# Loading Silu's table behind the norm's factor column, and spreading layer 0's factor a quarter of v later

## The chip, the cores and the metric

The kernel runs on one core of a Trainium2 chip. The core has five engines with a queue of instructions each: TensorE (PE in the profile, its weight loads PEld), VectorE (DVE), ScalarE (ACT), GpSimd (POOL) and SyncE (SP, which here only issues DMAs). Each engine works off its own queue in order and waits where an input, made by another engine or a DMA, isn't there yet.

The metric is the device time of one execution in microseconds (us). The kernel before was run three times: 654.84, 662.47 and 654.04 us.

## What is computed

A decoder trunk of two layers on one sequence of 256 tokens, with model width 1024, 16 heads of 64, and an FFN of width 2816, all in float32. Layer 0 mixes tokens by attention with forget gates, layer 1 by block-sparse attention with a relative-position bias. Each layer is, in short:

```python
u = rmsnorm(h, attn_norm_g[i])
h = h + attention_i(u) @ w_o
u = rmsnorm(h, ffn_norm_g[i])
gu = u @ ffn_w_in[i]
h = h + (silu(gu[..., :D_FF]) * gu[..., D_FF:]) @ ffn_w_out[i]
gate = sigmoid(rmsnorm(h, ple_norm_g[i]) @ ple_w_gate[i])
h = h + gate * (p[i] @ ple_w_up[i])
```

and a last rmsnorm makes the output. The norm is `y = x * rsqrt(mean(x*x) + eps) * g`: one factor for each token, and one gain for each feature.

## The kernel before

**Layout and precision.** Activations are kept feature by token: `h` is 128 partitions x 8 tiles x 256 tokens. Each float32 operand is split in a high part, rounded to a shorter format (`whi`, or `hi` of an activation), and a low part, the rest (`wlo`, `lo`); a product is then three matmuls, high x high, high x low and low x high (`mm3`, lines 90 to 92). For each weight tile of 128 x 1024 SP loads it into `raw` (six buffers), ACT rounds it to `whi` (line 152) and DVE subtracts it to `wlo` (line 153); `whi` and `wlo` have six buffers each, so this runs some tiles ahead of TensorE.

**The norm.** `Norm` works around the factor's late arrival. The matmuls run on h times gain alone (`block`, `pair`), without the factor. The factor comes later: `square` sums the squares on ACT and DVE, and `root` (line 207) sums over the partitions with two tiny matmuls into the bank `ss`, brings mean and epsilon together on DVE (`ms`), and raises it to the power -0.5 on POOL, into `col` (line 216): one factor for each token, tokens on the partitions. Where tokens lie along the free dimension, the factor has to be laid out as a row on all partitions: `spread` (line 218) multiplies the column, broadcast, by the identity on TensorE into the bank `pr`, and copies the bank twice into `row`, scaled on ACT (line 226) and plain on DVE (line 227).

**Layer 0's v and forget gates.** `attention` (line 381) first computes v with a loop over c = 0 to 3, two weight tiles each: a quarter of v's reduction per turn, 24 matmuls of 512 columns. In layer 0, at the end of the turn c = 1, `mid` (this is `fox_bias`) multiplies out the forget gates into the bank `pf`, the four squares run, and then `root`, `spread(-0.125)` and `small(done)`; the last issues three small loads on ACT's queue, behind the last square. After the loop `rest()` makes the gates' running sum from `pf` and `row` by a chain of DVE and ACT operations (lines 320 to 334), and v is copied out of its banks times `col` (line 414). In layer 1 `root` stands at the end of c = 2 and `spread` behind the whole loop. The projections of q and k then multiply by `row` (line 437), and the scores add the forget gates' sum (line 338).

**The FFN.** `ffn` (line 566) goes over 22 feature tiles f. The first two are computed together in `up([0, 1])`: four weight tiles, a loop over k, then `nm.root()` (line 583). `up([2])` then runs one weight tile (24 matmuls), `spread` (line 593), and `gated(*early)` for f = 0 and 1. `gated` multiplies the bank by the row into `gut` (DVE, line 600), applies Silu into `sg` (ACT, line 603), multiplies by the other half (DVE, line 604), and splits the product into high and low (`fp`, ACT line 261 and DVE line 262). `down(f)` then multiplies it into the banks `fo`.

**ACT's tables.** ACT evaluates a function by a table; the compiler puts a load of the table (ACT_TABLE_LOAD) ahead of the first operation that needs another one. `table(func, after)` (line 100) is an activation of one column into a scratch column, `warm`, whose only purpose is to have the load at that place; with `after` it reads the column given, and so waits for it. It is used for Exp at the start and behind the running sum, and for Sigmoid in both gates, right behind their `root` (lines 686 and 724). For Silu there is none: the load stands ahead of the first Silu of each layer.

**What sets the order.** A planner orders each engine's queue. It takes instructions in the order of the program where their inputs are ready by its own estimate, and lets a later one go ahead where an earlier one's input isn't. So an engine's queue follows the program only nearly: TensorE's two products of layer 0's spread stand two matmuls of v behind those of `ss`, though they follow directly in the program. `tc.issue_after` binds an instruction behind another on its engine.

Of the kernel before, what the change touches and what calls it, by code (L numbers as in the profile page):

```python
# [29 lines left out]
AF = mybir.ActivationFunctionType  # L30
# [41 lines left out]
def trunk(ctx: ExitStack, tc: tile.TileContext, xh, xg, wx, xr, pt, w, cst, gf, rel, hot, rvm, out):  # L72
# [7 lines left out]
    def bank(name):  # L80
        return ps.tile([P, 512], F32, tag="bank", name=name)
# [6 lines left out]
    def mm3(o, a, b, start, stop):  # L88
        (ah, al), (bh, bl) = a, b
        mm(o, ah, bh, start=start, stop=False, skip_group_check=True)  # L90
        mm(o, ah, bl, start=False, stop=False, skip_group_check=True)  # L91
        mm(o, al, bh, start=False, stop=stop, skip_group_check=True)  # L92
# [7 lines left out]
    def table(func, after=None):  # L100

        nc.scalar.activation(warm, ones if after is None else after, func)
# [20 lines left out]
    def half(at=0, entry=0):  # L123


        i = state["next"]
        state["next"] += 1
        if i not in (1, 2):
            raw = work.tile([P, HW + LINE], F32, tag="raw", bufs=RAW, name=f"raw{i}")
        ht, lt = (work.tile([P, HW + 2 * LINE], F32R, tag=n, bufs=6, name=f"{n}{i}") for n in ("whi", "wlo"))  # L130
        hi, lo = ht[:, at:at + HW], lt[:, at:at + HW]
        if entry:
            nc.sync.dma_start(raw[:, 0:HW], w[i - 2][:, 0:HW])
            nc.scalar.activation(hi, raw[:, 0:HW], AF.Copy)
            ats = [(at + FURTHER, 0, entry), (at + LINE, entry, HW)]
            for a, c0, c1 in ats:
                nc.vector.tensor_tensor(lt[:, a + c0:a + c1], raw[:, c0:c1], f32(hi[:, c0:c1]), op=ALU.subtract)
            return hi, [lt[:, a + k * P:a + (k + 1) * P] for a, c0, c1 in ats for k in range(c0 // P, c1 // P)]
        if i in (1, 2):
            raw = hw[:, i - 1, S:]  # L140
        parts = 2 if i < 2 else 1
        for q in range(parts):
            c = slice(q * HW // parts, (q + 1) * HW // parts)
            if i in (1, 2):
                at = slice(c.start + (S if q else 0), c.stop + S)
                nc.sync.dma_start(hw[:, i - 1, at], wx[i - 1][:, at])
            else:
                nc.sync.dma_start(raw[:, c], w[max(i - 2, 0)][:, c])
            if i + q == 0:
                nc.vector.tensor_copy(hi[:, c], raw[:, c])  # L150
            else:
                nc.scalar.activation(hi[:, c], raw[:, c], AF.Copy)  # L152
            nc.vector.tensor_tensor(lo[:, c], raw[:, c], f32(hi[:, c]), op=ALU.subtract)  # L153
        return hi, lo

    def blocks(entry=()):

        hi, lo = half(APART, len(entry) * P)
        return [[t[k] if isinstance(t, list) else t[:, k * P:(k + 1) * P] for k in range(KT)] for t in (hi, lo)]
# [72 lines left out]
    nm = Norm(0)  # L232
# [27 lines left out]
    def split(hi, lo, src):  # L260
        nc.scalar.activation(hi, src, AF.Copy)  # L261
        nc.vector.tensor_tensor(lo, src, f32(hi), op=ALU.subtract)  # L262

    def tokens(o, x, t, w, start, stop):

        at = slice(t * P, (t + 1) * P)
        mm3(o, (x[0][:, at], x[1][:, at]), w, start, stop)
# [10 lines left out]
    def residual(b, bk):  # L278
        at = h[:, 2 * b:2 * b + 2].rearrange("p k s -> p (k s)")
        nc.vector.tensor_tensor(at, at, bk, op=ALU.add)  # L280

    def feat(bks, m, w, x, start, stop):

        mm3(bks[m // 2][:, m % 2 * S:(m % 2 + 1) * S], w, x, start and m % 2 == 0, stop)
# [3 lines left out]
    def small(after):  # L288
        with tc.issue_after(after.ins):
            for t, a in ((rl, rel), (ht, hot), (rm, rvm)):  # L290
                nc.scalar.dma_start(t, a)
# [81 lines left out]
    def enter(bks, x, w):  # L373

        for hf in range(2):
            for a, b in ((0, 0), (1, 0), (0, 1)):
                for t in range(2):
                    mm(bks[2 * t + hf], x[a][:, t * P:(t + 1) * P], w[b][:, hf * HC:(hf + 1) * HC],
                       start=a == b, stop=False, skip_group_check=True)

    def attention(layer, nm, mid, early, nf):
        vb = [bank(f"v{layer}_{b}") for b in range(4)]
        rest = None
        for c in range(4):
            wt = [early.pop(0) if early else half() for _ in range(2)]
            for kk in range(2):
                hi, lo = wt[kk]
                k = 2 * c + kk
                if early and k == 0:
                    enter(vb, nm.k(0), wt[0])  # L390
                    continue
                for t in range(2):
                    for hf in range(2):
                        cols = slice(hf * HC, (hf + 1) * HC)
                        tokens(vb[2 * t + hf], nm.k(k), t, (hi[:, cols], lo[:, cols]), k == 0, k == KT - 1)
            if layer == 0 and c == 1:
                rest = mid(nm)
                for b in range(4):
                    done = nm.square(b)
                nm.root()  # L400
                nm.spread(-0.125)
                small(done)
            if layer == 1:
                moba[1](c)
            if layer == 1 and c == 2:
                nm.root()
# [159 lines left out]
    def ffn(layer, nm, filler, np_):  # L566
        acc = []
        prod = {}

        def up(fs):  # L570

            bks = {f: bank(f"gu{layer}_{f}") for f in fs}

            def step(f, a, wt, k, start):
                mm3(bks[f][:, a * S:(a + 1) * S], (wt[0][k], wt[1][k]), nm.k(k), start, k == KT - 1)

            if fs[0] == 0:
                wts = {f: (blocks(), blocks()) for f in fs}
                for k in range(KT):
                    for f in fs:  # L580
                        for a in range(2):
                            step(f, a, wts[f][a], k, k == 0 and a == 0)
                nm.root()
                return fs, bks
            for a in range(2):
                if fs[0] == 2 and a:
                    wt = gapped()
                else:
                    wt = blocks()
                for k in range(KT):  # L590
                    step(fs[0], a, wt, k, k == 0)
                if fs[0] == 2 and a == 0:
                    nm.spread()
                    gated(*early)
            gated(fs, bks)

        def gated(fs, bks):
            for f in fs:
                t = work.tile([P, 2, S], F32, tag="t2k", bufs=3, name=f"gut{layer}_{f}")
                nc.vector.tensor_tensor(t.rearrange("p a s -> p (a s)"), bks[f],  # L600
                                        nm.row.rearrange("p a s -> p (a s)"), op=ALU.mult)
                sg = work.tile([P, S], F32, tag="sg", name=f"sg{layer}_{f}")
                nc.scalar.activation(sg, t[:, 0], AF.Silu)
                nc.vector.tensor_tensor(sg, sg, t[:, 1], op=ALU.mult)  # L604
                both = work.tile([P, 2, S], F32R, tag="fp", bufs=4, name=f"fp{layer}_{f}")
                split(both[:, 0], both[:, 1], sg)
                prod[f] = both[:, 0], both[:, 1]

        def down(f):
            hi, lo = blocks()  # L610
            for m in range(KT):
                feat(acc, m, (hi[m], lo[m]), prod[f], f == 0, False)

        early = up([0, 1])
        acc.extend(bank(f"fo{layer}_{b}") for b in range(4))
        for f in range(2, FT, 2):
            up([f])
            up([f + 1])
            if f == FT - 6:
                pp = filler()  # L620
            if f < FT - 2:
                down(f - 2)
                down(f - 1)
        filler(pp)
        for b in range(4):
            hi, lo = blocks()
            for i in range(4):
                for n in range(2):
                    w = hi[2 * i + n], lo[2 * i + n]
                    feat(acc, 2 * b + n, w, prod[FT - 4 + i], False, i == 3)  # L630
            residual(b, acc[b])
            np_.pair(b)
        for b in range(4):
            np_.square(b)
# [163 lines left out]
    for layer in range(2):  # L798
# [8 lines left out]
        if layer == 0:  # L807
            nm = Norm(3)
# [126 lines left out]
```

## Time and profile before

| | us |
|---|---|
| runs | 654.84, 662.47, 654.04 (median 654.84) |
| profiled execution, its own time | 660.64 |
| its span, first to last instruction | 658.6 |
| TensorE busy in the span | 648.4 |
| weight loads (PEld) busy | 627.1 |
| DVE busy | 450.9 |
| ACT busy | 374.4 |
| POOL busy | 13.6 |

The profile is of one execution; times within it are from the start of its span. TensorE was granted 0.997 of its clock. A row of a timeline has the start, the duration, the engine, the line of the kernel, the operation with output and inputs, and the number of like operations that were merged; in brackets the idle time of the engine before it and what ended it. Back-to-back operations overlap a little, so durations in a row can add up to more than the distance of the starts. The rows of waits have who waited, on which line, for whom, the time in all, how often, and the longest.

The places that the change touches are early in layer 0 (from 16 to 45 us) and the start of each FFN (from 124 to 145 us, and from 440 to 461 us).

### The profile page before, as it was taken

What the parts mean: (1) busy time and instruction counts of PE and PEld (TensorE: products, weight loads), DVE (VectorE), ACT (ScalarE), POOL (GpSimd) and SP (SyncE); (2) the same over time, 40 slices, a digit from 0 to 9 for tenths busy, and PEclk for the clock granted to TensorE, in tenths of its full rate; (3) what the DMA queues carried; (4) which work ended last, traced back from release to release, by engine and by line L of the source; (5) the groups of instructions that cost most, each with busy time, mean ns of one, the idle gap of its engine ahead of it and who ended that gap; (6) DMA issues with size and microseconds to landing.
All of it is one profiled execution on the core that took longest, in us unless ns stands there. A gap on an engine that the chain in (4) does not pass through costs nothing.

```text
span 658.6 us, 13220 instructions
## 1 busy us (share of the span) xinstructions
PE 648.4 (98%) x5392; PEld 627.1 (95%) x5392; DVE 450.9 (68%) x723; ACT 374.4 (57%) x634; POOL 13.6 (2%) x21
## 2 busy tenths in 40 slices
PE   9999999999999999999999999999999999999995
PEld 7799999999999999999989999999999999999984
DVE  6788884786666666667796888568666556566765
ACT  6676674664444445455865677557444444444763
POOL 1000000000000000000001000000000000000001
PEclk9999999999999999999999999999999999999998
DMA  9888544386666666656487544447656656666501
GB/s 348 289 276 264 202 128 159 101 262 191 192 195 201 189 196 217 192 166 192 161 292 261 182 135 128 130 128 229 190 188 190 180 182 190 191 209 186 166 1 64
DMA packets 35883, 124.15 MB, mean 189 GB/s; under 512 B 3888, under 2 KB 6256, under 8 KB 35696
## 3 DMA queue, kind: packets, MB, share of 16 engines
q1 hardware_dynamic: 35408, 122.92, 58.8%
q8 instruction: 42, 0.69, 0.4%
q10 hardware_dynamic: 416, 0.40, 0.2%
q14 instruction: 17, 0.14, 0.1%
HBM read 122.24 MB, written 4.22 MB: 192 GB/s over the span
## 4 chain that ended last, share of the span: by engine, by line
PE 95%; issue 3%; ACT 1%; DVE 1%; POOL 0%; POOLq 0%; ACTq 0%
PE gu L90 12%; PE gu L92 12%; PE gu L91 12%; PE fo L91 6%; PE fo L92 6%; PE fo L90 6%; PE pq L90 5%; PE pq L91 4%; PE pq L92 4%; PE wo L90 2%; PE wo L91 2%; PE wo L92 2%; PE v L90 2%; PE v L92 2%; PE v L91 2%
## 5 line engine op out<-in xcount | busy, mean ns | idle before, releaser
L153 DVE TENSOR_TENSOR wlo<-raw,whi 128x1024 fp32r<-128x1024 f32 (+1 forms) x207 | 251.2, 1219 | 131.8 <-ACT whi L152 131.4
L152 ACT ACTIVATE whi<-raw 128x1024 fp32r<-128x1024 f32 (+1 forms) x206 | 216.0, 1055 | 181.4 <-PE gu L91 79.1
L90 PE MATMUL gu<-g,whi 128*128 128x256 f32 x704 | 196.2, 279 | 0.0
L92 PE MATMUL gu<-g,wlo 128*128 128x256 f32 x704 | 195.8, 278 | 0.0
L91 PE MATMUL gu<-g,whi 128*128 128x256 f32 x704 | 195.8, 278 | 0.0
L91 PEld LDWEIGHTS gu<-g,whi 128*128 128x128 f32 x704 | 133.5, 190 | 0.0
L90 PEld LDWEIGHTS gu<-g,whi 128*128 128x128 f32 x704 | 132.2, 188 | 0.0
L92 PEld LDWEIGHTS gu<-g,wlo 128*128 128x128 f32 x704 | 132.2, 188 | 0.0
L91 PE MATMUL fo<-fp,whi 128*128 128x256 f32 x352 | 98.3, 279 | 0.1
L92 PE MATMUL fo<-fp,wlo 128*128 128x256 f32 x352 | 98.0, 279 | 0.0
L90 PE MATMUL fo<-fp,whi 128*128 128x256 f32 x352 | 98.0, 278 | 0.0
L90 PE MATMUL pq<-g,whi 128*128 128x256 f32 x256 | 71.7, 280 | 0.0
L91 PE MATMUL pq<-g,whi 128*128 128x256 f32 x256 | 71.0, 277 | 0.0
L92 PE MATMUL pq<-g,wlo 128*128 128x256 f32 x256 | 71.0, 277 | 0.0
L91 PEld LDWEIGHTS fo<-fp,whi 128*128 128x128 f32 x352 | 66.8, 190 | 0.6 <-DVE fp L262 0.5
L90 PEld LDWEIGHTS fo<-fp,whi 128*128 128x128 f32 x352 | 66.1, 188 | 0.0
L92 PEld LDWEIGHTS fo<-fp,wlo 128*128 128x128 f32 x352 | 66.1, 188 | 0.0
L90 PEld LDWEIGHTS pq<-g,whi 128*128 128x128 f32 x256 | 48.2, 188 | 1.1 <-issue 0.6
L91 PEld LDWEIGHTS pq<-g,whi 128*128 128x128 f32 x256 | 48.2, 188 | 0.0
L92 PEld LDWEIGHTS pq<-g,wlo 128*128 128x128 f32 x256 | 48.1, 188 | 0.0
L261 ACT ACTIVATE fp<-sg 128x256 fp32r<-128x256 f32 x44 | 18.1, 415 | 45.9 <-DVE sg L604 45.9
L600 DVE TENSOR_TENSOR gut<-gu,row 128x512 f32<-128x512 f32 x44 | 30.0, 690 | 14.8 <-PE gu L92 14.8
(176 smaller groups left out, 970.2 us busy)
## 6 DMA issues: line engine op xcount, KB each, us to landing
raw<-w SPq DMA_DIRECT2D x206, 512.0 KB, 4.3
raw<-w SPq DMA_DIRECT2D x7, 540.0 KB, 5.2
d<-d SPq DMA_DIRECT2D x4, 768.0 KB, 9.7
bias<-d SPq DMA_DIRECT2D x4, 512.0 KB, 6.7
h<-xh SPq DMA_DIRECT2D x1, 1024.0 KB, 9.9
hw<-wx SPq DMA_DIRECT2D x1, 640.0 KB, 5.8
hw<-xr SPq DMA_DIRECT2D x1, 640.0 KB, 7.7
raw<-w SPq DMA_DIRECT2D x2, 256.0 KB, 3.2
```

The source lines that it names most:

```text
L90: mm(o, ah, bh, start=start, stop=False, skip_group_check=True)
L91: mm(o, ah, bl, start=False, stop=False, skip_group_check=True)
L92: mm(o, al, bh, start=False, stop=stop, skip_group_check=True)
L152: nc.scalar.activation(hi[:, c], raw[:, c], AF.Copy)
L153: nc.vector.tensor_tensor(lo[:, c], raw[:, c], f32(hi[:, c]), op=ALU.subtract)
L261: nc.scalar.activation(hi, src, AF.Copy)
L600: nc.vector.tensor_tensor(t.rearrange("p a s -> p (a s)"), bks[f], nm.row.rearrange("p a s -> p (a s)"), op=ALU.mult)
```

## The change

Two edits:

- In layer 0, `spread(-0.125)` moves from the end of the turn c = 1 to the end of the turn c = 2: in the program its two products, and the two copies into `row`, now stand behind the 24 matmuls of that quarter of v. `root` and `small(done)` stay at the end of c = 1.
- In `up([0, 1])`, behind `root`, `table(AF.Silu, nm.col[:, 0:1])` is added: an activation of one column that reads the norm's factor column. It is there once in each layer's FFN.

```diff
@@ attention
                 for b in range(4):
                     done = nm.square(b)
                 nm.root()
+                small(done)
+            if layer == 0 and c == 2:
                 nm.spread(-0.125)
-                small(done)
             if layer == 1:
                 moba[1](c)
             if layer == 1 and c == 2:
@@ ffn, up
                         for a in range(2):
                             step(f, a, wts[f][a], k, k == 0 and a == 0)
                 nm.root()
+                table(AF.Silu, nm.col[:, 0:1])
                 return fs, bks
             for a in range(2):
                 if fs[0] == 2 and a:
```

## The prediction

> **What bounds the kernel now.** I read the busy shares and the chain that ended last, then who TensorE waited for, and then the timelines of the places the change touches, engine by engine. From the page:
>
> ```profile
> span 658.6 us, 13220 instructions
> PE 648.4 (98%) x5392; PEld 627.1 (95%) x5392; DVE 450.9 (68%) x723; ACT 374.4 (57%) x634; POOL 13.6 (2%) x21
> PE 95%; issue 3%; ACT 1%; DVE 1%; POOL 0%; POOLq 0%; ACTq 0%
> ```
>
> TensorE is the bound: 98% busy, 95% of the chain. The change removes no matmul, so it can only win time in which TensorE stands still: 658.6 - 648.4 = 10.2 us in all. The waits of TensorE's weight loads name the two places that the change touches:
>
> ```profile
> PEld pr L223 <- POOL col L216: 1.8, 1, 1.8
> PEld fo L91 <- DVE fp L262: 0.5, 2, 0.3
> ```
>
> One wait for the factor column in layer 0, and two short ones, one in each FFN, for the first product's low half. Everything the change can directly win is in these two rows.
>
> **Part A, the spread of layer 0, a quarter of v later.** TensorE's timeline around it (start, duration, idle before in brackets), then POOL, ACT and DVE at the same place:
>
> ```profile
> 20.98 0.39 PE L91 MATMUL v<-wlo,g 128*128 128x512 f32 x1
> 21.21 0.50 PE L212 MATMUL ss<-first_line,sq 128*128 128x1 f32 x4
> 21.57 0.49 PE L92 MATMUL v<-whi,g 128*128 128x512 f32 x1
> 21.90 0.40 PE L91 MATMUL v<-wlo,g 128*128 128x512 f32 x1
> 23.67 0.71 PE L223 MATMUL pr<-con,col 128*128 128x128 f32 x4 [1.38 <-POOL col L216]
> 24.14 0.48 PE L92 MATMUL v<-whi,g 128*128 128x512 f32 x1
> ```
>
> ```profile
> 22.06 1.56 POOL L216 TENSOR_TENSOR col<-ms,nhalf 128x2 f32<-128x2 f32 x1 [9.72 <-DVE ms L214]
> ```
>
> ```profile
> 18.68 1.04 ACT L152 ACTIVATE whi<-raw 128x1024 fp32r<-128x1024 f32 x1
> 24.42 0.38 ACT L226 ACTIVATE row<-pr 128x256 f32<-128x256 f32 x1 [4.69 <-PE pr L223]
> ```
>
> ```profile
> 21.83 2.36 DVE L153 TENSOR_TENSOR wlo<-raw,whi 128x1024 fp32r<-128x1024 f32 x2
> ```
>
> The products pr stand two v matmuls behind ss on TensorE, but POOL needs until 22.06 + 1.56 = 23.62 for the column. A v matmul follows the last one after 21.21 - 20.98 = 0.23 us; so without pr the next would start at 21.90 + 0.23 = 22.13 instead of waiting to 23.67: a stall of 1.54 us (the row's 1.38 counts from the modelled end). The four pr records themselves take 24.14 - 23.67 = 0.47 us; that is moved, not removed.
>
> After the change 24 v matmuls of two weight tiles (k = 4 and 5) rank ahead of pr, and 15 of them (3 of k = 4, 12 of k = 5) are still to run at 21.57, which is 15 x 0.23 = 3.4 us: pr comes at about 25.1, 1.5 us after the column. Is the work that fills the hole ready? The weights' high parts are (ACT finished k = 5 and 6 by 19.72 and then stood for 4.69 us); the low part of k = 5 is the first of the two subtractions at 21.83, ready at about 21.83 + 2.36/2 = 23.0, and TensorE asks for it after the rest of k = 4 and the four matmuls by whi of k = 5, at 22.13 + 0.23 + 4 x 0.23 = 23.3. So the fill holds with 0.3 us to spare. Layer 1 already has its spread a quarter of v behind its root, and there pr waits for nothing:
>
> ```profile
> 349.44 0.61 PE L223 MATMUL pr<-con,col 128*128 128x128 f32 x4
> ```
>
> What is late then: the row (ACT copy, DVE copy) about 1.5 us later, hence the forget-gate chain behind it, which ends in the cast of c on POOL and is first read by the scores:
>
> ```profile
> 36.48 0.29 POOL L334 CAST c<-c 128x128 fp32r<-128x128 f32 x1 [12.87 <-DVE c L333]
> ```
>
> ```profile
> 44.34 0.33 PE L338 MATMUL sp<-c,sel 64*128 64x384 f32 x2
> ```
>
> There are 44.34 - 36.77 = 7.6 us of cover; a gain of 1.5 and a row 1.5 us later leave some 4.6. On ACT's queue the conversion of k = 7 is no longer bound to stand behind the row's copy; if it still does, it starts 1.5 us later, at about 26.2, its subtraction ends near 28.5, and TensorE asks for that low half at about 25.6 + 12 x 0.23 + 0.23 = 28.6. Tight, but covered. The three small loads of `small` keep their place behind the last square, ahead of the row's copy, on ACT's queue; SP's and POOL's lists are not touched. A: -1.54. Its bounds are 0 (pr is put back where it was) and -1.8 (all that the weight-load row shows); I take -1.54, since it comes from the spacing of the matmuls themselves.
>
> **Part B, Silu's table.** ACT, POOL, DVE and TensorE in the FFN of layer 0:
>
> ```profile
> 127.89 3.91 ACT L152 ACTIVATE whi<-raw 128x1024 fp32r<-128x1024 f32 x4 [5.00 <-PE gu L91]
> 132.18 1.06 ACT L152 ACTIVATE whi<-raw 128x1024 fp32r<-128x1024 f32 x1 [0.38 <-PE gu L91]
> 133.14 0.36 ACT L226 ACTIVATE row<-pr 128x256 f32<-128x256 f32 x1
> 135.39 1.07 ACT L152 ACTIVATE whi<-raw 128x1024 fp32r<-128x1024 f32 x1 [1.88 <-PE gu L91]
> 136.47 1.28 ACT L603 ACT_TABLE_LOAD   x1
> 137.77 0.73 ACT L603 ACTIVATE sg<-gut 128x256 f32<-128x256 f32 x2
> 138.40 1.05 ACT L152 ACTIVATE whi<-raw 128x1024 fp32r<-128x1024 f32 x1
> ```
>
> ```profile
> 130.36 1.61 POOL L216 TENSOR_TENSOR col<-ms,nhalf 128x2 f32<-128x2 f32 x1 [93.59 <-DVE ms L214]
> ```
>
> ```profile
> 128.98 1.23 DVE L153 TENSOR_TENSOR wlo<-raw,whi 128x1024 fp32r<-128x1024 f32 x1 [3.97 <-ACT whi L152]
> ```
>
> ```profile
> 135.07 1.88 DVE L600 TENSOR_TENSOR gut<-gu,row 128x512 f32<-128x512 f32 x3
> 136.86 1.21 DVE L153 TENSOR_TENSOR wlo<-raw,whi 128x1024 fp32r<-128x1024 f32 x1
> 138.22 0.76 DVE L604 TENSOR_TENSOR sg<-sg,gut 128x256 f32<-128x256 f32 x2
> 139.48 1.23 DVE L153 TENSOR_TENSOR wlo<-raw,whi 128x1024 fp32r<-128x1024 f32 x1 [0.49 <-ACT whi L152]
> 140.62 0.75 DVE L262 TENSOR_TENSOR fp<-sg,fp 128x256 fp32r<-128x256 f32 x2
> ```
>
> ```profile
> 140.74 0.28 PE L90 MATMUL fo<-fp,whi 128*128 128x256 f32 x1
> 141.09 0.39 PE L91 MATMUL fo<-fp,whi 128*128 128x256 f32 x1
> ```
>
> The load (1.28 us) stands ahead of the first Silu, and TensorE then waits: half of the 0.5 us in the waits row above, 0.25 us per layer, is all that a perfect move can win. But DVE, not ACT alone, carries this stretch: from 128.98 to 140.62 it rests only where the load has held ACT. With 1.14 us between a subtraction and the next start (140.62 - 139.48) those rests are 138.22 - 138.00 = 0.22 and, taking the pair at 138.22 as 0.67 less overlap, 139.48 - 138.89 = 0.59: 0.81 us to reclaim.
>
> What does the load cost at its new place? The gates of layer 0 have the same form already (four weight tiles, root, table on the column, one more tile, spread), with Sigmoid:
>
> ```profile
> 314.26 2.96 ACT L152 ACTIVATE whi<-raw 128x1024 fp32r<-128x1024 f32 x3 [6.94 <-PE pg L91]
> 317.23 1.28 ACT L102 ACT_TABLE_LOAD   x1
> 318.53 0.20 ACT L102 ACTIVATE first_line<-col 128x1 f32<-128x1 f32 x1
> ```
>
> ```profile
> 315.35 1.23 DVE L153 TENSOR_TENSOR wlo<-raw,whi 128x1024 fp32r<-128x1024 f32 x1 [5.91 <-ACT whi L152]
> ...
> 322.32 1.88 DVE L674 TENSOR_TENSOR pgt<-pg,row 128x512 f32<-128x512 f32 x3
> ```
>
> There the load falls behind the third of four conversions, and DVE's first product by the row starts 322.32 - 315.35 = 6.97 us behind its first subtraction; in the FFN it is 135.07 - 128.98 = 6.09. So the load at its new place delays DVE by 0.88 us. Behind it on ACT's queue stand the fourth conversion (a tile for o, not needed before 140.74), the next one and the row's copy; behind those on DVE the four subtractions' last, the row's second copy and gut; SP's next loads into raw come as much later, with several tiles in hand. The wait on col is covered: the load ends at about 130.83 + 1.28 = 132.11 and the column is there at 130.36 + 1.61 = 131.97. Later the 0.81 us come back, so fp's low half moves by 0.88 - 0.81 = +0.07 us per layer, +0.15 for both. The added activation (0.20 us, twice) lies in ACT's idle time of 1.88 us. Bounds: -0.5 (both stalls gone) and +1.8 (twice 0.88, nothing reclaimed); I take +0.15, from the nearest row, the Sigmoid load.
>
> The Trainium skill (ScalarE: Activation LUTs, What ACT_TABLE_LOAD costs) adds a drain of about 1380 ns to the 1283 ns of each load. The trace has the 1.28 us but no drain: the next activation starts 0.02 us behind the load, in the FFN and in the gates. By the page's total of 2.66 us the early load would hold ACT 1.38 us longer in each layer, an estimate of +2.8 us over both, and the sum would be +1.4 instead of -1.4.
>
> **The sum.** -1.54 + 0.15 = -1.4 us. The profiled execution took 660.64 us, its span 658.6; they would become 659.2 and 657.2. It is slower than the median of the runs, 654.84 (654.04 to 662.47), by a difference that lies in no stage of the change; against the median I predict 654.84 - 1.4 = 653.4.
>
> **The rivals.**
> 1. Both parts pay in full: the load slips into idle time and DVE loses nothing. -1.54 - 0.48 = -2.0: 652.8. Against it: the 0.88 us of the gates.
> 2. The move does nothing: the planner orders by when it believes inputs ready (pr stands two matmuls behind ss, though POOL takes 1.56 us) and puts pr into a gap that it sees early, right behind the four whi matmuls of k = 5 or sooner. A falls toward 0, B stays: 655.0. For it: TensorE's order there is the planner's, not the program's. Against it: in layer 1 a lower rank was enough.
> 3. Slower: the load goes behind the second conversion instead of the third. ACT then waits for the column to 131.97, the third conversion ends at about 133.1 instead of 130.8, and gut starts near 136.9, 1.83 us later instead of 0.88; with 0.81 reclaimed each layer loses 1.0, so -1.54 + 2.0 = +0.5: 655.3; one conversion earlier still, 657.5. It decides from gut 1.6 us late, where 2 x (1.6 - 0.81) exceeds A. Against it: the same distance of 1.1 us from the first conversion to ss in gates and FFN.
> 4. The load holds ACT for longer than its row shows, as by a drain. If that doubled it, 2 x 1.28 us would be added: 656.0. Against it: the 0.02 us behind each load.
>
> **How the numbers follow.** My forecast has 5 in 10, the first rival 1.5, the second 1.5, the third 1.2, the fourth 0.2; 0.6 is left for another order further on. All of them lie within 4 us, less than what separates two runs of one kernel here. So the range is set by these: from the fastest run with the full gain, 654.04 - 2.0 = 652.0, to the profiled execution with the third rival's loss, 660.64 + 0.5 = 661.1. Two per cent, about what a measurement of this kernel can tell from no change, is 13.1 us; no case reaches it, so faster has 0.01, slower 0.02, and within it 0.97.
>
> **What would show it.** Right: the row "pr from col" is gone from TensorE's waits, v matmuls follow ss without a gap, and the ACT idle of 4.69 us ahead of the row's copy is gone; in each FFN the load stands behind three conversions on L102, gut starts about 0.9 us later against the first subtraction, and the wait of fo for fp is still there at 0.25 to 0.4 us. Wrong: pr still waiting for the column, a new wait of v for wlo at k = 5 or 7, gut more than 1.6 us late, or fo waiting for nothing.

## The result, and the profile after

Twenty executions of the changed kernel took 653.59 us in the median (652.74 to 654.11). Twenty of the kernel before, taken beside them, took 655.46 (654.04 to 663.6). The ratio is 0.9939 (95% interval 0.9913 to 0.9965): faster by about 0.6%, clear of no change, and under the 2% that was named beforehand. I had forecast 653.4 us and a difference of 0.2%. Ratios, here and below, are of means, and leave out executions more than 1.5% above the fastest of their kernel.

The medians hide the form of the difference. The executions of the kernel before lie on two levels: 13 of the 20 between 654.04 and 656.75, seven between 660.31 and 663.6. All 20 of the changed kernel lie within 1.4 us. The means are 657.55 and 653.56, 4.0 us apart. The profiled execution of before (660.64 us) was one of the upper level; that of the changed kernel took 654.03.

The page of the changed kernel, its span and the busy time of each engine:

```profile
span 652.0 us, 13223 instructions
PE 642.4 (99%) x5392; PEld 620.9 (95%) x5392; DVE 450.4 (69%) x723; ACT 375.3 (58%) x636; POOL 13.6 (2%) x21
```

The span fell by 6.6 us (658.6 to 652.0), and TensorE's busy time by 6.0 (648.4 to 642.4), with the same 5392 matmuls. So the time in which TensorE stood still fell by only 0.6 us, from 10.2 to 9.6; the rest is that its matmuls took less time. No sum over waits can show that.

**Where it went.** TensorE's timeline where layer 1's FFN starts and ends its products, before:

```profile
456.73 0.28 PE L90 MATMUL fo<-fp,whi 128*128 128x256 f32 x1
457.08 0.38 PE L91 MATMUL fo<-fp,whi 128*128 128x256 f32 x1
457.31 0.28 PE L92 MATMUL fo<-fp,wlo 128*128 128x256 f32 x1
...
609.71 0.40 PE L90 MATMUL pu<-whi,phi 128*128 128x512 f32 x1
```

And after:

```profile
456.43 0.28 PE L90 MATMUL fo<-fp,whi 128*128 128x256 f32 x1
456.55 0.28 PE L91 MATMUL fo<-fp,whi 128*128 128x256 f32 x1
456.66 0.28 PE L92 MATMUL fo<-fp,wlo 128*128 128x256 f32 x1
...
603.31 0.40 PE L90 MATMUL pu<-whi,phi 128*128 128x512 f32 x1
```

Before, the second product `fo` waits for `fp`, and the three products take 457.31 - 456.73 = 0.58 us against 0.23 after: the wait costs 0.35 us. But from the first `fo` to the first `pu` it is 152.98 us before and 146.88 after: 6.10 less, of which the wait explains 0.35. The other 5.75 us are spread evenly over the FFN. TensorE's windows (stretch, its length, busy time and number of matmuls, granted clock, DMA share, GB/s) show it. The first row is in layer 0's FFN, the two others in layer 1's; before:

```profile
160.00:180.00 20.00, 20.00 (x179) 1.00 0.61 188
485.00:505.00 20.00, 20.00 (x172) 1.00 0.62 186
560.00:580.00 20.00, 20.00 (x172) 1.00 0.67 203
```

After:

```profile
160.00:180.00 20.00, 20.00 (x179) 1.00 0.61 189
485.00:505.00 20.00, 20.00 (x179) 1.00 0.66 199
560.00:580.00 20.00, 20.00 (x179) 1.00 0.68 202
```

At the same granted clock of 1.00, and with TensorE busy throughout, the same matmuls run 172 to a window in the one and 179 in the other. (A window also counts the two or three that reach into it.) From start to start that is 0.118 us against 0.113, 4%. Some 1300 matmuls (152.98 / 0.118) times 4.5 ns are the 5.8 us. In this window layer 0 ran at 0.113 in both profiles. So TensorE has two steady rhythms here, and layer 1 of the profiled execution of before fell into the slower one where `fo` had waited.

The slower rhythm is no rarity. It also stands, for a short while, at the start of every FFN, between the small products `ss` of `root` and the products `pr` of `spread`. TensorE before, in layer 0, behind `ss` (which starts at 128.83 us):

```profile
129.39 0.28 PE L91 MATMUL gu<-g,whi 128*128 128x256 f32 x1
...
131.98 0.28 PE L92 MATMUL gu<-g,wlo 128*128 128x256 f32 x1
132.10 0.64 PE L223 MATMUL pr<-con,col 128*128 128x128 f32 x4
...
132.69 0.28 PE L91 MATMUL gu<-g,whi 128*128 128x256 f32 x1
...
140.29 0.28 PE L92 MATMUL gu<-g,wlo 128*128 128x256 f32 x1
```

From 129.39 to 131.98 us there are 22 distances of 0.118 us, and from 132.69 to 140.29 there are 67 of 0.113. The 13 profiles of this document have 26 FFNs. In all 26 the row of matmuls goes over to the slower rhythm at `ss`, and in 23 it is back on the faster one behind `pr`.

**Part A.** The changed kernel's TensorE around the spread:

```profile
21.54 0.50 PE L212 MATMUL ss<-first_line,sq 128*128 128x1 f32 x4
...
22.46 0.40 PE L92 MATMUL v<-whi,g 128*128 128x512 f32 x1
23.99 0.49 PE L223 MATMUL pr<-con,col 128*128 128x128 f32 x2 [1.14 <-POOL col L216]
24.24 1.17 PE L90 MATMUL v<-whi,g 128*128 128x512 f32 x4
25.24 0.38 PE L223 MATMUL pr<-con,col 128*128 128x128 f32 x2
...
43.77 0.49 PE L451 MATMUL sp<-qkt 64*128 64x128 f32 x4
```

The spread's two products have come apart. The first stands one v matmul later than before and still waits for `col`; the second stands behind the four products by `whi` of k = 5. From `ss` to the first scores it is 43.77 - 21.54 = 22.23 us. Before, the scores' first row was

```profile
43.66 0.49 PE L450 MATMUL sp<-qkt 64*128 64x128 f32 x4
```

which is 43.66 - 21.21 = 22.45 us behind its `ss`. The move won 0.22 us where I had forecast 1.54.

**Part B.** ACT of the changed kernel in layer 0's FFN:

```profile
127.99 2.96 ACT L152 ACTIVATE whi<-raw 128x1024 fp32r<-128x1024 f32 x3 [5.00 <-PE gu L91]
130.96 1.28 ACT L102 ACT_TABLE_LOAD   x1
132.25 0.20 ACT L102 ACTIVATE first_line<-col 128x1 f32<-128x1 f32 x1
```

DVE at the same place:

```profile
129.08 1.23 DVE L153 TENSOR_TENSOR wlo<-raw,whi 128x1024 fp32r<-128x1024 f32 x1 [3.96 <-ACT whi L152]
...
136.05 1.28 DVE L602 TENSOR_TENSOR gut<-gu,row 128x512 f32<-128x512 f32 x2
137.25 0.42 DVE L606 TENSOR_TENSOR sg<-sg,gut 128x256 f32<-128x256 f32 x1
137.58 0.69 DVE L602 TENSOR_TENSOR gut<-gu,row 128x512 f32<-128x512 f32 x1
138.18 0.42 DVE L262 TENSOR_TENSOR fp<-sg,fp 128x256 fp32r<-128x256 f32 x1
```

And TensorE:

```profile
140.84 0.28 PE L90 MATMUL fo<-fp,whi 128*128 128x256 f32 x1
140.95 0.28 PE L91 MATMUL fo<-fp,whi 128*128 128x256 f32 x1
```

The load stands behind three conversions, and `gut` starts 136.05 - 129.08 = 6.97 us behind the first subtraction: exactly the gates' distance, 0.88 more than before. What follows on DVE is another order, though. Before it was three `gut`, a subtraction, both `sg`, another subtraction and then `fp`, at 140.62. Now the chain of f = 0 goes straight through, two `gut`, `sg`, `gut`, `fp`, and `fp` starts at 138.18, 2.8 us ahead of the product that reads it (140.95). `fo` waits for nothing, in both layers.

### The profile page after: what moved, and what is told of

Same layout as the page of the kernel before. It is cut to its first block, busy times and chain, and to the rows that moved or that the text cites. A ratio compares the mean times of both kernels' runs of the same rounds, so it can differ in the third digit from the quotient of the medians.

```text
span 652.0 us, 13223 instructions
## 1 busy us (share of the span) xinstructions
PE 642.4 (99%) x5392; PEld 620.9 (95%) x5392; DVE 450.4 (69%) x723; ACT 375.3 (58%) x636; POOL 13.6 (2%) x21
## 4 chain that ended last, share of the span: by engine, by line
PE 96%; issue 3%; ACT 0%; POOL 0%; POOLq 0%; DVE 0%; ACTq 0%
PE gu L92 12%; PE gu L90 12%; PE gu L91 12%; PE fo L92 6%; PE fo L90 6%; PE fo L91 6%; PE pq L90 5%; PE pq L92 5%; PE pq L91 4%; PE wo L90 2%; PE wo L91 2%; PE wo L92 2%; PE v L90 2%; PE v L91 2%; PE v L92 2%
```

## The experiments

All ran beside the kernel before. Over all of this, 129 executions of the kernel before are on record; 80 took up to 657.61 us, and 49 from 659.86 up, three of these over 667. "Upper" below means 658.5 us or more. The medians and the counts have all executions.

| run | median (lowest to highest, n) | upper | ratio to before |
|---|---|---|---|
| changed kernel | 653.59 (652.74 to 654.11, 20) | 0 | 0.9939 [0.9913, 0.9965] |
| e1, table alone | 654.29 (653.44 to 655.56, 12) | 0 | 0.9958 [0.9926, 0.9989] |
| e2, spread alone | 655.04 (653.95 to 666.96, 12) | 5 | 1.0012 [0.9975, 1.0048] |
| e3, spread bound | 652.43 (651.82 to 652.94, 12) | 0 | 0.993 [0.99, 0.996] |
| e4, table in layer 1 alone | 654.87 (654.07 to 656.51, 12) | 0 | 0.9964 [0.993, 0.9998] |
| e5, table in layer 0 alone | 654.9 (653.99 to 667.41, 12) | 2 | 0.9957 [0.9921, 0.9994] |
| e6, low half late by 3.1 us | 660.49 (658.2 to 665.93, 12) | see text | 1.0049 [1.0006, 1.0092] |
| e7, column later | 656.8 (655.72 to 658.2, 12) | 0 | 0.9974 [0.9939, 1.0008] |
| e8, low half late by 1.1 us | 661.98 (654.63 to 667.95, 12) | 10 | 1.0024 [0.9975, 1.0074] |
| e9, break in layer 1 | 659.55 (658.37 to 665.59, 12) | see text | 1.0028 [0.9992, 1.0063] |
| e10, changed kernel again | 653.79 (653.37 to 660.81, 12) | 1 | 0.9942 [0.9907, 0.9978] |
| e11, e3 again | 652.37 (651.5 to 652.9, 12) | 0 | 0.9923 [0.9891, 0.9954] |

### Each part alone (e1 and e2)

e1 is the kernel before with the table's line, e2 the kernel before with the spread moved:

```diff
 e1: in up([0, 1])
                 nm.root()
+                table(AF.Silu, nm.col[:, 0:1])
 e2: in attention
+                small(done)
+            if layer == 0 and c == 2:
                 nm.spread(-0.125)
-                small(done)
```

> The Silu table alone; layer 0's spread stays behind c = 1. Theory (the low half of fp no longer makes fo wait, and with that wait TensorE's drop into its slower matmul rhythm, 117.8 instead of 113.3 ns, in layer 1's FFN is gone): no row of fo waiting for fp; 113.3 ns from 455 to 600 us; every execution between 652.5 and 654.5 us, none near 661; median 653.5, like the changed kernel. Rival (the shift of the spread is what keeps the slower rhythm away): two levels as before, near 654.5 and 661, the upper one in about 8 of 20.

> The later spread alone, no Silu table. Theory: fo waits for fp in both layers as before, 0.25 us each; two levels as before, near 654.5 and 661, the upper in a third or so of the executions; pr still waits for the column, 1.0 to 1.6 us. Rival (the spread keeps the slower rhythm away): one level, at 653 to 654.

The table alone took the upper level away: 0 of 12 against 49 of 129. The spread alone did not: 5 of 12, and its lower executions, 654.64 in the median, stand 0.5 us below the 655.1 of the kernel before. For the upper level both theories hold. e1's times came out higher than expected: the median is 0.8 us above the 653.5 expected, and five executions lie above 654.5. In e1's profile another cost of the old place of the spread showed up. TensorE's windows there:

```profile
24.00:26.00 2.00, 2.00 (x8) 0.59 0.82 260
26.00:28.00 2.00, 2.00 (x6) 0.55 0.75 238
28.00:30.00 2.00, 2.00 (x11) 1.00 0.78 199
```

The fourth column is the granted clock. Behind the wait for `col` it falls to 0.59 and 0.55 for the better part of 4 us, and six to eight v matmuls run in 2 us instead of ten to twelve. Neither profile of before and after has this drop; e4's has it. So the old place costs more than its wait in some executions.

### The spread where the diff says (e3 and e11)

The changed kernel, with the spread's instructions bound behind the last matmul of the turn c = 2 (`mm3` and `tokens` are made to return their last matmul):

```diff
-                        tokens(vb[2 * t + hf], nm.k(k), t, ...)
+                        last = tokens(vb[2 * t + hf], nm.k(k), t, ...)
...
             if layer == 0 and c == 2:
-                nm.spread(-0.125)
+                with tc.issue_after(last.ins):
+                    nm.spread(-0.125)
```

> The changed kernel with both pr products bound behind the last v matmul of c = 2 (issue_after on TensorE), so that the planner cannot put one of them into an earlier gap. Theory (the changed kernel's part A gains nothing, since one pr product still waits for the column): no wait of pr for the column; 1.2 to 1.5 us faster than the changed kernel, median 652.2. Rival (the v matmuls behind it then wait for their low halves on DVE instead, or the forget-gate chain is late): no gain, 653.5.

> e3 once more, on the same chip as e10. Theory (part A pays once both products are behind the quarter of v): 1.2 to 1.4 us below e10, as the distance from ss to the first scores (22.23 against 20.82 us) says. Rival (e3's lower time came from another chip): same as e10 within 0.3 us.

TensorE's timeline of e3:

```profile
21.58 0.50 PE L212 MATMUL ss<-first_line,sq 128*128 128x1 f32 x4
...
25.25 0.39 PE L92 MATMUL v<-whi,g 128*128 128x512 f32 x1
25.48 0.61 PE L223 MATMUL pr<-con,col 128*128 128x128 f32 x4
...
42.41 0.49 PE L452 MATMUL sp<-qkt 64*128 64x128 f32 x4
```

Both products stand together behind the quarter of v and wait for nothing. From `ss` to the first scores it is 42.41 - 21.58 = 20.83 us: 1.62 less than before, 1.40 less than in the changed kernel. The medians follow: 652.43 against the 653.59 of the result, which were measured apart, and 652.37 against 653.79, which were measured together on one chip. This is the fastest of the versions measured. The prediction's price for the move was right; the diff alone did not make the move.

### The table in one layer only (e4 and e5)

Both take e1 and load the table early in one of the layers:

```diff
                 nm.root()
-                table(AF.Silu, nm.col[:, 0:1])
+                if layer == 1:        # e4;  layer == 0 in e5
+                    table(AF.Silu, nm.col[:, 0:1])
```

> The Silu table in layer 1's FFN only, spread as before. Theory, if the drop into the slower rhythm happens in layer 1 only: one level, about 0.2 us over the table in both layers, 653.7. If the wait in layer 0 can cause it too, its FFN has some 1400 matmuls behind that wait: an upper level some 6 us higher in a part of the executions.

> The Silu table in layer 0's FFN only, spread as before. Theory (the wait of fo for fp in layer 1 is what can drop TensorE into the slower rhythm of 117.8 ns until the FFN ends): the upper level near 661 is back, in a third or so of the executions; the lower one near 654.7. Rival (the table as such, in either layer, keeps it away): one level near 654.7.

With the wait gone from layer 1 alone, none of 12 is on the upper level. Its median of 654.87 is 1.2 above what I expected; the four executions from 656.18 up have a mean granted clock of 0.993 or 0.994, as e1's two with the clock drop. That layer 0's wait by itself does not bring the upper level rests on these 12 executions, since no other kernel here keeps that wait alone. With the wait gone from layer 0 alone, two are: 661.52 and 667.41. Two of 12 is fewer than the kernel before has (49 of 129), but too few to tell the two shares apart. What speaks more is the profile of the execution at 667.41, which has 173 matmuls at 160 to 180 us and 172 at 485 to 505: both layers on the slower rhythm. In layer 0, where `fo` does not wait, the slower rhythm of the stretch behind `ss` stayed on behind `pr`. So the wait is not the only place that decides.

### A wait put back (e6 and e8)

The changed kernel, with the low half of layer 1's first `fp` held back by a short chain on POOL. Two of its columns are multiplied by one, so the values stay; e6 multiplies five times, e8 once:

```diff
+        def late(lo):
+            one2 = tiny.tile([P, 2], F32, bufs=1, name="one2")
+            nc.gpsimd.tensor_scalar(one2, f32(lo), 0.0, 1.0, op0=ALU.mult, op1=ALU.add)
+            nc.gpsimd.tensor_tensor(one2, one2, nhalf, op=ALU.pow)
+            for _ in range(5):        # once in e8
+                nc.gpsimd.tensor_tensor(lo, f32(lo), one2, op=ALU.mult)
...
+                if layer == 1 and f == 0:
+                    late(both[:, 1, 0:2])
```

> The changed kernel, tables in both layers, but in layer 1 the low half of f = 0 passes through seven small POOL operations that multiply two of its columns by one, some 2.8 us, so that fo has to wait for it again, by 0.2 to 0.7 us; TensorE, ACT and DVE have the same instructions in the same order as in the changed kernel. Theory (the wait itself, not the place of the table, causes the slower rhythm): an upper level some 6 us over the lower appears in a third or so of the executions; the lower one near 654.0. Rival (it hangs on the order of ACT and DVE): one level, near 654.0.

> As e6, with one POOL multiplication of the low half instead of five, so that fo waits some 0.4 us in layer 1 instead of 3.1, and the granted clock has no reason to fall. Order of TensorE, ACT and DVE as in the changed kernel. Theory (a short wait of fo is enough to start the slower rhythm): lower level 653.6 to 654.3, upper level some 5.75 us above it, in 2 to 7 of 12. Rival (it takes the long wait, or the old order of DVE and ACT): one level at 653.6 to 654.3.

e6's chain was longer than meant, since the five multiplications of two columns took 3.30 us on POOL: `fo` waited for 3.1 us, and the clock fell to 0.57 in the window from 460 to 464 us. Its 12 executions form two groups of six, 658.2 to 658.64 and 662.35 to 665.93. The first holds the wait and the clock drop, and the profiled execution, one of this group (658.31), has layer 1 on the faster rhythm, with 179 matmuls at 485 to 505 us: a long wait need not start the slower one. The second group has more, but e6 mixes too much to be read.

e8 has the wait without the clock drop. Its wait, in the waits of TensorE's weight loads:

```profile
PEld fo L91 <- POOL fp L603: 1.1, 1, 1.1
```

Ten of 12 executions lie above 659.9, and two at 654.63 and 655.65; the last are near what the changed kernel and 1.1 us give (654.7). So two executions lie 1 to 2 us above the changed kernel's median, and ten lie 6 to 14 above it, where I had expected 2 to 7 of 12. The windows of the profiled one, at 667.95:

```profile
160.00:180.00 20.00, 20.00 (x173) 1.00 0.58 184
485.00:505.00 20.00, 20.00 (x172) 1.00 0.57 185
```

The granted clock is 1.00 in both, so this is no drop of the clock. This execution had both layers on the slower rhythm, as e5's had: in layer 0 it stayed on behind `pr`, and in layer 1 it was gone behind `pr` and came back at the added wait. Of the other nine only the time is known, so in which layer each of them was slow is not shown. But layer 0 has the changed kernel's code, and that kernel has one upper execution in 32 (e10), so I put most of the ten down to the wait in layer 1.

### The column later still (e7)

e1, with layer 0's factor column computed twice on POOL, the first time into a column that nobody reads, so that the old spread waits longer:

```diff
+            if n == 0:
+                twice = tiny.tile([P, 2], F32, bufs=1, name="twice")
+                nc.gpsimd.tensor_tensor(twice, ms, nhalf, op=ALU.pow)
             nc.gpsimd.tensor_tensor(self.col, ms, nhalf, op=ALU.pow)
```

> The table in both layers, spread as before, and layer 0's first column is computed twice on POOL, one behind the other, so that pr waits 1.56 us longer, about 3.1 us in all. Theory (the wait for the column can make the granted clock fall to about 0.55 for some 3.4 us behind it, which costs 1.6 us and happened in part of the executions of the kernels that have the 1.5 us wait): now nearly every execution pays it: 654.3 + 1.6 + 1.0 to 2.0, median about 657, clock well under 1 between 25 and 30 us. Rival (the wait costs its length alone): 655.9 and a clock of 1.00.

It costs 2.5 us against e1 (656.8 to 654.29), where the second power adds 1.5. TensorE's windows:

```profile
24.00:26.00 2.00, 1.17 (x6) 0.83 0.90 264
26.00:28.00 2.00, 2.00 (x6) 0.50 0.82 250
28.00:30.00 2.00, 2.00 (x9) 0.82 0.45 76
```

The clock drop is there again. The mean granted clock of each execution says how often: in e7 it is 0.992 to 0.995 in ten of 12, and 0.996 in the two fastest (655.72 and 655.84), which lie where e1's executions without a drop and 1.5 us more would lie (654.14, their median, + 1.5). In e1 it is 0.994 in two of 12 and 0.996 or 0.997 in the others. So a wait of 2.5 us, which is what TensorE's row shows here, seems to bring the drop in most executions, and the one of 1.4 us in e1 in few.

### A break without a wait (e9)

The kernel before, with two more products like the spread's ahead of f = 10 in layer 1, into a bank that nobody reads. It asks whether any interruption of the row of matmuls sets the rhythm anew:

```diff
         for f in range(2, FT, 2):
+            if layer == 1 and f == 10:
+                pause = bank("pause")
+                for t in range(2):
+                    mm(pause[:, t * P:(t + 1) * P], nm.col[:, t:t + 1].to_broadcast([P, P]), ident, start=True, stop=True)
             up([f])
```

> The kernel before with two more products like those of the spread, whose result nobody reads, ahead of f = 10 in layer 1's FFN. Theory (the rhythm only lasts until something interrupts the row of like matmuls, and products like pr bring back the faster one, as they do ahead of f = 2): the lower level 0.5 us over that of before, 655.5; the upper one only 2.5 to 3 us above the lower, near 658.5, instead of 6 to 7. Rival (the rhythm is set for the whole FFN by something else): upper level near 661.5 to 662.5 as before.

It does, but the other way. TensorE's windows ahead of the two products and behind them:

```profile
485.00:505.00 20.00, 20.00 (x179) 1.00 0.62 190
520.00:540.00 20.00, 20.00 (x172) 1.00 0.57 186
```

The rhythm was the faster one, and at the products (511.30 us) it went over to the slower one and stayed there to the end of the FFN. No execution was faster than 658.37, so the break seems to bring the slower rhythm in nearly every execution: some 800 matmuls follow it, and 4.5 ns more for each are 3.6 us (an estimate) over the 655.1 of before's lower level. An interruption sets the rhythm, and it needs no wait. Products of this form bring back the faster rhythm in 23 of 26 FFNs, where `ss` had left the slower one; here they found the faster one and left the slower. I had seen only the first half of this.

### The changed kernel again (e10)

> The changed kernel once more, beside e11. Theory: in layer 1 nothing interrupts the row of matmuls between the spread and the FFN's end, so no execution lies 5 to 7 us above the rest on that account. What e5 and e8 leave open is layer 0, where their profiles have the slower rhythm from the spread's products on, with no wait of fo: if the changed kernel can fall into it there too, some executions lie 6.8 us above the rest (near 660.5). Lower level 653.0 to 654.3.

One of 12 was on the upper level, and it is the profiled one, at 660.81. Its windows:

```profile
160.00:180.00 20.00, 20.00 (x172) 1.00 0.55 188
485.00:505.00 20.00, 20.00 (x179) 1.00 0.60 190
```

Layer 0 is on the slower rhythm and layer 1 on the faster one. As in every FFN here, the slower one came at `ss` (129.16 us); this time `pr` (132.43 us) did not end it, and it lasted to the end of layer 0's FFN. So the changed kernel can still be caught, at another interruption, once in 32 executions.

Over all kernels whose layer 1 has no wait of `fo` (the changed one, e1, e3, e4, e7, e10, e11), 1 of 92 executions was upper. With that wait (before, e2, e5, e8), 66 of 165 were. e6 and e9, which have it and another disturbance besides, are not counted.

## Why the prediction was right or wrong

**The time was near by luck, and the difference was not near.** The forecast of 653.4 us lies 0.2 from the median, but the two kernels differ by three times what I gave. Of the two terms of the sum, one came out at a seventh of its size and the other with the wrong sign, and their errors cancel in part. The step that failed is the bound at the start: "The change removes no matmul, so it can only win time in which TensorE stands still". Of the 6.6 us between the spans, only 0.6 are time in which TensorE stood still; 6.0 are matmuls that started at shorter distances. The same error stands in the sum, where the profiled execution is slower than the median "by a difference that lies in no stage of the change". It lay in layer 1's FFN, from the wait of `fo` on that part B removes, and is 5.75 us. The 5.8 us between that execution (660.64) and the median were in hand, and I put them down to the execution; the two windows of 172 and 179 matmuls were in the trace of before, and I had compared no like stretches of the two layers. The chances then held no case in which removing a wait of 0.25 us is worth more than 0.25 us.

**Part A: the mechanism right, the sum that of another rival.** TensorE's wait for the column is 1.54 us long, and removing it is worth about that: 1.62 us from `ss` to the scores in e3, 1.4 us between the medians of e11 and e10. The diff did not remove it, since the planner placed the two products on its own estimate, one behind k = 4 and one behind the four products by `whi` of k = 5. That is rival 2, down to the place it named, and a row of `pr` waiting for `col` is still there (1.14 us), as the prediction's signs of being wrong had it. Measured: -0.22 from `ss` to the scores, for -1.54 forecast, with 0 as the bound. The argument that in layer 1 a lower rank was enough did not carry over. The cover was as reckoned: in e3 no wait for `wlo` appears between `ss` and `pr`, and the row 1.5 us later delays nothing up to the scores. What I had not priced is the clock behind the wait; it adds some 1.6 us in single executions of the old place (e1's profile: 24.04 us from `ss` to the scores, 45.47 - 21.43, against 22.45).

**Part B: the delay right, the consequence of the wrong sign.** `gut` came later by the 0.88 us taken from the gates. The error is in "Later the 0.81 us come back, so fp's low half moves by 0.88 - 0.81 = +0.07 us per layer": that kept DVE's order. The new activation changed it, in both layers; e1 has the changed kernel's order on DVE, e2 that of before. Against the first subtraction `fp` came 2.5 us earlier (138.18 - 129.08 = 9.10 for 140.62 - 128.98 = 11.64) instead of 0.07 later, and the wait of 0.35 us in each layer went: -0.7 for +0.15. "Fo waiting for nothing" stood in the prediction as a sign that it was wrong, and that sign came. Rival 1, both in full, had that half of it.

**No sign of the drain.** The Trainium skill (ScalarE: Activation LUTs, What ACT_TABLE_LOAD costs) would have put 1.38 us more on ACT; in the changed kernel the activation starts at 132.25, 0.01 us behind the load's end at 130.96 + 1.28 = 132.24. Rivals 3 and 4 fell with the rows above.

**The sum.** By stages of the profile: 0.2 (A) + 0.7 (B's two waits) + 5.75 (rhythm of layer 1) = 6.7, against the spans' 6.6. For the typical execution of before, on its lower level, the rhythm's term is absent and 0.9 is left; 655.1 - 653.6 = 1.5 was measured there. I have no row for the 0.6 between them. Clock drops are little of it: the mean granted clock is on record for 67 of the 80 lower executions of before, and the 55 that have 0.996 or more, as all of the changed kernel have, still have a median of 654.98, which is 1.4 above 653.59.

**What stays open.** What decides, at an interruption, which of the two rhythms follows. With the short wait of before 49 of 129 executions were upper, and with 1.1 us in e8 10 of 12. Behind the short wait in layer 1, two of the four profiles that have it go on at the slower rhythm (before, e5) and two at the faster (e2, e9); in layer 0, behind the same short wait, all four that have it (before, e2, e4, e9) go on at the faster one. Whether each of the 49 upper executions of before had layer 1 on the slower rhythm is known of one profile alone; that removing the wait removes the level (e4, e1) and adding one brings it back (e8) was measured.

## What to carry to other kernels

Before a prediction, lay like stretches of the trace side by side (the two layers, or two windows of one loop) and compare the matmuls in each: an equal busy share and an equal granted clock can hide 4%, and a profiled execution that is slower than the median is to be explained from its own rows. A short wait of TensorE can cost far more than its length, by what follows it; where the slowest executions matter, removing a wait of 0.3 us can be worth several. And where a planner orders the queue, moving a line is a request: what decides is the order of the rows afterwards, and a bound instruction (e3) is the way to have the move.

## What was unexpected of the hardware

**Two rhythms at a granted clock of 1.00.** A row of 128x256 matmuls starts every 0.113 us or every 0.118 us, and keeps to one of them for 150 us and more. In the 13 profiles the change from one to the other was seen only at interruptions, and in both directions: to the slower one at `ss` in 26 of 26 FFNs, at two products of another form (e9), and at three of ten waits of `fo` (before, e5, e8); back to the faster one at `pr` in 23 of 26. It costs 5.75 us over layer 1's FFN, and some 7 us over layer 0's from `pr` on (660.81 us against a median of 653.76 for the other 11 of e10). The Trainium skill (TensorE: Matmul & The Clock Gate, Wait — 56ns, not 53.3ns?) gives N / 2.4 GHz and about 2.5 ns for the distance of warm matmuls, 109 ns for 256 columns as an estimate from it; both measured rhythms are longer, and that section has one distance for a warm clock, not two.

**The clock falls behind short waits.** A wait of 1.4 us for `col`, by TensorE's row, brought it to 0.54 to 0.61 in the profiles of e1 and e4, and the same wait did not in that of before; waits of 2.5 us (e7) and 2.9 us (e6) did it in theirs. The drop lasts about 3 to 4 us. The Trainium skill (TensorE: Matmul & The Clock Gate, What's actually happening) has the clock throttled after an idle window of about 3.4 us, with the windows running free of the kernel, and released after a busy one of the same length. The length of the drop agrees. The length of the wait does not: 1.4 us, less than half of that window, was enough at times. Why it was, no run here shows.
